# A convolution mixer's layer norm: four channel blocks added on VectorE before one product with ones, and one small load moved to ScalarE's queue

## The chip, the cores and the metric

The kernel runs on one core of one Trainium2 chip. The metric is the device time of one launch in microseconds (us). Names used below: TensorE (PE; its weight loads are PEld), VectorE (DVE), ScalarE (ACT), GpSimd (POOL) and SyncE (SP, which issues most DMAs). Every engine works through its own queue of instructions strictly in order and waits on semaphores for the others.

## The reference, cut to what matters

Two decoder layers over 256 tokens of width 1024. Each has four mixers on one projection of the normed input, then a feed-forward part (dense in layer 0, eight routed experts in layer 1). The change touches the fourth mixer, a gated depthwise convolution over 512 channels with a layer norm behind it:

```
def _conv_mixer(za, zg, w, bias, ln_g, ln_b):
    y = za * jax.nn.sigmoid(zg)
    y = lax.conv_general_dilated(y, w[:, None, :], window_strides=(1,), ...)   # 31 causal taps
    y = y + bias
    return jax.nn.silu(_layer_norm(y, ln_g, ln_b))

def _layer_norm(x, g, b):
    xc = x - jnp.mean(x, axis=-1, keepdims=True)
    y = xc * lax.rsqrt(jnp.mean(xc * xc, axis=-1, keepdims=True) + EPS)
    return y * g + b
```

The means run over the 512 channels of a token.

## The kernel before, in words

All large products are float32 by three passes: an operand is split into a rounded high part and a remainder, and `mm3` (lines 196 to 198) issues high by high, high by low and low by high. Weights come in pieces of 1 MB: SP issues the DMA into `raw` (line 163), ScalarE makes the high part `wh` (line 164), VectorE the low part `wl` (line 171), which is 128x2048 and waits for `wh`. There are three buffers each of `wh` and `wl`, so ScalarE starts a new `wh` only when TensorE has done with an older piece. `fill()` loads pieces until three are ahead of the products, and `get()` calls it.

Three engines, PE, ACT and DVE, run in the order in which the program issues their instructions. Beside the products of a layer's mixers run small generators ("threads"): `products()` gets its piece first, and so puts that piece's `wh` and `wl` on the queues of ScalarE and VectorE, and after every second `kk` it calls `tick()`, which lets each thread issue its next step and pops some convolution taps (line 503, VectorE, 128x256 each). `conv_norm` is such a thread. It waits until all taps are issued and then works on `cacc`, which holds the convolution as 128 channels by 4 blocks by 256 tokens:

1. the sum over all 512 channels as four products of `ones` with the four blocks, added up in the PSUM tile `cs` (line 757); ScalarE scales it to `cmean` (line 759); VectorE subtracts it (line 760); ScalarE squares into `c2` (line 762);
2. four ticks later the same four products on the squares (line 766), from which ScalarE makes `csd` (line 768);
3. two ticks later VectorE takes the reciprocal (line 770), scales (lines 771, 773), ScalarE takes a tanh (line 775), and after two more steps `oh` and `ol`, the split result, are made (lines 214, 215).

Around it run `merge(1, 1, gt)` (products on `oh`, `ol` of another mixer, then lines 697 and 698 on VectorE), `gates()` (products on the normed input `hh`, `hl`, then the tanh `gt` of line 685 on ScalarE) and `merge(0, ...)`. PSUM tiles of these products, `zps`, rotate over four buffers, so a later `gates()` starts when ScalarE has read an older tile into `gt`. In layer 1 the same code runs again some 536 us later.

At the start of the kernel SP loads the two halves of the first token tile `x_sb` (line 83), and GpSimd's queue loads `col`, the column vectors of both layers (gains, biases, taps; 128x320, line 89), then `pos_i` (line 91) and `inv` (line 93). TensorE transposes `x_sb` with `ident` (line 243), VectorE multiplies by the gain in `col` to give `xg` (line 261), and ScalarE and VectorE split that for the first products.

Of the kernel before, what the change touches and what calls it, by code (L numbers as in the profile page):

```python
# [11 lines left out]
F32 = mybir.dt.float32  # L12
# [4 lines left out]
OP = mybir.AluOpType  # L17
AX = mybir.AxisListType
# [3 lines left out]
P = 128  # L22
D = 1024
S = 256
# [40 lines left out]
def trunk(ctx: ExitStack, tc: tile.TileContext, x, pos, invf, rows, cols, wst, w_a, w_kvf, w_gate, w_br,  # L65
          w_out, f_g, f_u, f_d, router, e_g, e_u, e_d, gfin, out):
    nc = tc.nc
# [18 lines left out]
    ident = const.tile([P, P], F32, name="ident")  # L86
    make_identity(nc, ident)
    col = dconst.tile([P, L, NCOL], F32, name="col")
    nc.gpsimd.dma_start(col, cols)
    pos_i = const.tile([P, NT], I32, name="pos_i")  # L90
    nc.gpsimd.dma_start(pos_i, pos.rearrange("o (t p) -> p (o t)", p=P))
    inv = dconst.tile([P, HD // 2], F32, name="inv")
# [2 lines left out]
    ones = const.tile([P, P], F32, name="ones")  # L95
# [116 lines left out]
    def split(hi, lo, src, scale=None):  # L212
        if scale is None:
            nc.scalar.activation(hi, src, AF.Copy)  # L214
            nc.vector.tensor_sub(lo, src, hi.bitcast(F32))  # L215
        else:
            nc.scalar.activation(hi, src, AF.Copy, scale=scale)
            nc.vector.scalar_tensor_tensor(lo, src, scale, hi.bitcast(F32), op0=OP.mult, op1=OP.subtract)
# [126 lines left out]
    def mixers(l, mine, head, following):  # L345
        with ExitStack() as c2:
            mp = c2.enter_context(tc.tile_pool(name=f"mp{l}", bufs=1, reuse_waits="tile"))
            wk = c2.enter_context(tc.tile_pool(name=f"wk{l}", bufs=2, reuse_waits="tile"))
            bp = c2.enter_context(tc.tile_pool(name=f"bp{l}", bufs=8, reuse_waits="tile"))
            pmm = c2.enter_context(tc.tile_pool(name=f"pmm{l}", bufs=4, space=PSUM, reuse_waits="tile"))  # L350
            psm = c2.enter_context(tc.tile_pool(name=f"psm{l}", bufs=4, space=PSUM, reuse_waits="tile"))

            def big(name, shape=(P, NT, W), dtype=F32):

                n = int(np.prod(shape[1:]))
                tl = bp.tile([P, 1056], dtype, tag="big", name=name)[:shape[0], :n]
                if len(shape) == 3:
                    return tl.rearrange("p (a b) -> p a b", a=shape[1])
                if len(shape) == 4:
                    return tl.rearrange("p (a b c) -> p a b c", a=shape[1], b=shape[2])  # L360
                return tl
# [132 lines left out]
            cacc = mp.tile([P, 4, S], F32, name="cacc")  # L494
# [78 lines left out]
            def new_oT(n):  # L573
                hi = mp.tile([P, 4, S], F32R, name="oh", tag="oh", bufs=2)
                lo = mp.tile([P, 4, S], F32R, name="ol", tag="ol", bufs=2)
                oT[n] = (hi, lo)
                return hi, lo
# [171 lines left out]
                    yield 1  # L749


            def conv_norm():
                while taps:
                    yield 1
                ps = psm.tile([P, S], F32, tag="sm", name="cs")
                for b in range(4):
                    nc.tensor.matmul(ps, ones, cacc[:, b], start=b == 0, stop=b == 3)
                mean = wk.tile([P, S], F32, name="cmean", tag="o")
                nc.scalar.activation(mean, ps, AF.Copy, scale=1.0 / W)
                nc.vector.tensor_tensor(cacc, cacc, mean[:, None, :].to_broadcast([P, 4, S]), OP.subtract)  # L760
                c2_ = big("c2", (P, 4, S))
                nc.scalar.activation(c2_, cacc, AF.Square)
                yield 4
                ps = psm.tile([P, S], F32, tag="sm", name="cs")
                for b in range(4):
                    nc.tensor.matmul(ps, ones, c2_[:, b], start=b == 0, stop=b == 3)
                sd = wk.tile([P, S], F32, name="csd", tag="o")
                nc.scalar.activation(sd, ps, AF.Sqrt, bias=epsc, scale=1.0 / W)
                yield 2
                nc.vector.reciprocal(sd, sd)  # L770
                nc.vector.tensor_tensor(cacc, cacc, sd[:, None, :].to_broadcast([P, 4, S]), OP.mult)
                for b in range(4):
                    nc.vector.tensor_scalar(cacc[:, b], cacc[:, b], col[:, l, C_CG + b:C_CG + b + 1],
                                            col[:, l, C_CBB + b:C_CBB + b + 1], op0=OP.mult, op1=OP.add)
                nc.scalar.activation(c2_, cacc, AF.Tanh, scale=0.5)
                yield 2

                nc.vector.tensor_scalar(c2_, c2_, 1.0, 0.5, op0=OP.add, op1=OP.mult)
                nc.vector.tensor_mul(cacc, cacc, c2_)
                yield 1  # L780
                while 1 in oT:
                    yield 1
                oh, ol = new_oT(3)
                split(oh, ol, cacc)
# [74 lines left out]
            merge(1, 1, gt)  # L859
            del oT[1]  # L860
            start(conv_norm())
            for dc in range(2):
                gt = gates()
# [186 lines left out]
    def experts(l, mine):  # L1050
# [3 lines left out]
        with ExitStack() as c2:  # L1054
# [379 lines left out]
            with tc.If(nc.values_load(over_i[0:1, NE:NE + 1], min_val=0, max_val=1) > 0):  # L1434
# [8 lines left out]
    heads = [Normed(col[:, 0, C_MIX:C_MIX + KD]), Normed(col[:, 0, C_FFN:C_FFN + KD]),  # L1443
             Normed(col[:, 1, C_MIX:C_MIX + KD]), Routed(1)]
    mixers(0, heads[0], heads[1], [f_g[0, 0, h] for h in range(2)])
    dense_ffn(0, heads[1], heads[2], [w_a[1, CA, h] for h in range(2)])
    mixers(1, heads[2], heads[3], [e_g[0, 0, 0], e_g[0, 0, 1], e_u[0, 0, 0]])
    dense_ctx.close()
    experts(1, heads[3])
# [68 lines left out]
```

## Time and profile before

| what | value |
|---|---|
| three runs | 1726.6, 1728.15, 1728.6 us; median 1728.15 |
| the profiled execution | 1726.18 us, span 1724.4 us |
| PE busy | 1675.1 us, 97% of the span |
| PEld busy | 1215.4 us, 70% |
| DVE busy | 1054.3 us, 61% |
| ACT busy | 830.5 us, 48% |
| POOL busy | 12.1 us, 1% |
| bytes moved | 497.69 MB, mean 289 GB/s |
| granted TensorE clock, mean | 0.989 |

Times in the rows count from the start of the span; the profiled execution's own time has 1.8 us around the span. A duration is from an instruction's start to its end; neighbours on one engine overlap a little at their ends, so the step from one start to the next says what an instruction takes of the engine's time. A bracket at the end of a row holds the idle time of that engine before the instruction and what ended it.

### The profile page before, as it was taken

How to read it: one execution, taken by the hardware profiler on the slowest of the kernel's cores; microseconds unless marked ns; L12 is line 12 of the kernel's file. 1: busy time of each engine (PE TensorE's matmuls, PEld its weight loads, DVE VectorE, ACT ScalarE, POOL GpSimd, SP SyncE). 2: the span in 40 equal slices, each digit the busy share in tenths (PEclk: the TensorE clock that was granted, in tenths of full speed). 3: DMA queues.
4: the chain of work that ended last, by engine and by line, in shares of the span. 5: the costliest groups of instructions: out<-in, count | busy, mean ns of one | idle time of the engine just before them, and what ended most of it. 6: DMA issues, size and time to landing. Idle time of an engine off the chain costs nothing.

```text
span 1724.4 us, 20366 instructions
## 1 busy us (share of the span) xinstructions
PE 1675.1 (97%) x7800; PEld 1215.4 (70%) x7800; DVE 1054.3 (61%) x1282; ACT 830.5 (48%) x884; POOL 12.1 (1%) x28
## 2 busy tenths in 40 slices
PE   8999999999999999999999999999999999999996
PEld 6888888888887888888776565656656565655652
DVE  6779976555545678986675455536456544735534
ACT  6656454544434566445474444435444443534433
POOL 1000000000000000000000000000000000000000
PEclk9999999999999999999899999999999999999998
DMA  7444445555553643454668999999999999999996
GB/s 274 171 147 146 172 149 193 196 185 181 176 190 123 244 147 123 171 183 175 277 244 322 421 421 422 421 421 418 416 421 421 421 421 421 421 421 421 421 397 231
DMA packets 77818, 497.69 MB, mean 289 GB/s; under 512 B 8752, under 2 KB 8800, under 8 KB 20368
## 3 DMA queue, kind: packets, MB, share of 16 engines
q1 hardware_dynamic: 76752, 493.45, 72.8%
q0 software_dynamic: 960, 2.85, 0.6%
q8 instruction: 63, 1.03, 0.2%
q14 instruction: 43, 0.35, 0.1%
HBM read 495.22 MB, written 1.05 MB: 288 GB/s over the span
## 4 chain that ended last, share of the span: by engine, by line
PE 47%; DMA 9%; DVE 4%; ACT 3%; issue 1%; ACTq 0%; SPq 0%; DVEq 0%
DMA raw<-in_e_d 5%; PE yps L1302 4%; PE gps L1302 4%; PE ups L1302 3%; PE zps L196 3%; PE zps L198 3%; PE zps L197 3%; PE gps L196 3%; PE gps L197 3%; PE yps L197 3%; DVE wl L171 3%; PE gps L198 2%; PE yps L196 2%; PE yps L198 2%; ACT wh L164 2%; PE ups L196 2%
## 5 line engine op out<-in xcount | busy, mean ns | idle before, releaser
L171 DVE TENSOR_TENSOR wl<-raw,wh 128x2048 fp32r<-128x2048 f32 (+1 forms) x312 | 681.9, 2195 | 342.4 <-ACT wh L164 342.2
L164 ACT ACTIVATE wh<-raw 128x2048 fp32r<-128x2048 f32 (+1 forms) x312 | 571.1, 1838 | 406.1 <-PE zps L198 76.4
L196 PE MATMUL zps<-wh,hh 128*128 128x512 f32 (+1 forms) x544 | 215.7, 397 | 2.9 <-ACT wh L214 1.7
L197 PE MATMUL zps<-wl,hh 128*128 128x512 f32 (+1 forms) x544 | 209.5, 385 | 0.9 <-DVE wl L215 0.9
L198 PE MATMUL zps<-wh,hl 128*128 128x512 f32 (+1 forms) x544 | 209.6, 385 | 0.0
L215 DVE TENSOR_TENSOR al<-ps_t,ah 128x512 fp32r<-128x512 f32 x42 | 28.4, 688 | 181.0 <-ACT ah L214 180.8
L196 PEld LDWEIGHTS zps<-wh,hh 128*128 128x128 f32 x544 | 102.7, 189 | 23.7 <-ACT wh L214 2.1
L1372 ACT ACTIVATE act<-gps 128x512 f32<-128x512 f32 x42 | 25.1, 598 | 195.0 <-PE gps L1302 171.7
L197 PEld LDWEIGHTS zps<-wl,hh 128*128 128x128 f32 x544 | 102.7, 189 | 21.4 <-DVE wl L215 2.5
L198 PEld LDWEIGHTS zps<-wh,hl 128*128 128x128 f32 x544 | 102.5, 188 | 20.7
L1302 PE MATMUL ups<-rawn,xs 128*64 128x512 f32 x448 | 101.6, 597 | 1.6 <-DMA rawn<-in_e_u 1.6
L503 DVE SCALAR_TENSOR_TENSOR cacc<-ypad,col,cacc 128x256 f32<-128x256 f32 x240 | 101.4, 478 | 0.0
L1302 PE MATMUL yps<-rawn,aT 128*64 128x512 f32 x448 | 100.3, 596 | 0.0
L1302 PE MATMUL gps<-rawn,xs 128*64 128x512 f32 x448 | 100.3, 596 | 0.0
L197 PE MATMUL yps<-wl,ah 128*128 128x512 f32 x224 | 91.4, 408 | 6.7 <-DVE wl L171 6.5
L196 PE MATMUL yps<-wh,ah 128*128 128x512 f32 x224 | 92.0, 411 | 2.0 <-ACT wh L164 2.0
L196 PE MATMUL ups<-wh,xb 128*128 128x512 f32 x224 | 91.6, 409 | 0.0
L197 PE MATMUL gps<-wl,xb 128*128 128x512 f32 x224 | 88.8, 397 | 2.2 <-DVE wl L171 2.0
L198 PE MATMUL yps<-wh,al 128*128 128x512 f32 x224 | 90.4, 404 | 0.0
L196 PE MATMUL gps<-wh,xb 128*128 128x512 f32 x224 | 90.1, 402 | 0.0
L198 PE MATMUL ups<-wh,xb 128*128 128x512 f32 x224 | 88.6, 395 | 0.0
L198 PE MATMUL gps<-wh,xb 128*128 128x512 f32 x224 | 88.4, 394 | 0.0
(311 smaller groups left out, 2408.6 us busy)
## 6 DMA issues: line engine op xcount, KB each, us to landing
raw<-in_e_g SPq DMA_DIRECT2D x56, 1024.0 KB, 13.6
raw<-in_e_u SPq DMA_DIRECT2D x56, 1024.0 KB, 13.6
raw<-in_e_d SPq DMA_DIRECT2D x54, 1024.0 KB, 11.9
rawn<-in_e_g SPq DMA_DIRECT2D x52, 1024.0 KB, 12.7
rawn<-in_e_u SPq DMA_DIRECT2D x52, 1024.0 KB, 16.2
rawn<-in_e_d SPq DMA_DIRECT2D x52, 1024.0 KB, 14.1
raw<-in_w_gate SPq DMA_DIRECT2D x32, 1024.0 KB, 4.7
raw<-in_w_a SPq DMA_DIRECT2D x28, 1024.0 KB, 4.8
```

The source lines that it names most:

```text
L164: nc.scalar.activation(hi[:, sl], raw[:, sl], AF.Copy)
L171: nc.vector.tensor_sub(lo[:, sl], raw[:, sl], hi[:, sl].bitcast(F32))
L196: nc.tensor.matmul(ps, xh, wh, start=first, stop=False)
L197: nc.tensor.matmul(ps, xh, wl, start=False, stop=False)
L198: nc.tensor.matmul(ps, xl, wh, start=False, stop=last)
L215: nc.vector.tensor_sub(lo, src, hi.bitcast(F32))
L503: nc.vector.scalar_tensor_tensor(cacc[:, b], src, wcol, cacc[:, b], op0=OP.mult, op1=OP.add)
L1302: nc.tensor.matmul(ps[js], lhs(k)[:, js], w[:, kk], start=k == 0, stop=k == ktot - 1)
L1372: nc.scalar.activation(a, gps, AF.Silu)
```

## The change

A helper adds the four blocks on VectorE (one reduce over the block axis, from 128x256x4 to 128x256 into `cb`) and multiplies the result once by `ones`. Both sums of the norm use it. `cb` takes its buffer from the pair that `cmean` and `csd` use. The load of `col` is issued by ScalarE's queue in place of GpSimd's.

```diff
@@ -86,7 +86,7 @@
     col = dconst.tile([P, L, NCOL], F32, name="col")
-    nc.gpsimd.dma_start(col, cols)
+    nc.scalar.dma_start(col, cols)
@@ -749,21 +749,25 @@
+            def over_channels(a):
+
+                cb = wk.tile([P, S], F32, name="cb", tag="o")
+                nc.vector.tensor_reduce(cb, a.rearrange("p b s -> p s b"), axis=AX.X, op=OP.add)
+                ps = psm.tile([P, S], F32, tag="sm", name="cs")
+                nc.tensor.matmul(ps, ones, cb, start=True, stop=True)
+                return ps
+
             def conv_norm():
                 while taps:
                     yield 1
-                ps = psm.tile([P, S], F32, tag="sm", name="cs")
-                for b in range(4):
-                    nc.tensor.matmul(ps, ones, cacc[:, b], start=b == 0, stop=b == 3)
+                ps = over_channels(cacc)
                 mean = wk.tile([P, S], F32, name="cmean", tag="o")
...
                 yield 4
-                ps = psm.tile([P, S], F32, tag="sm", name="cs")
-                for b in range(4):
-                    nc.tensor.matmul(ps, ones, c2_[:, b], start=b == 0, stop=b == 3)
+                ps = over_channels(c2_)
                 sd = wk.tile([P, S], F32, name="csd", tag="o")
```

On TensorE the products with ones keep their places between the same two `zps` products: four instructions on `cacc` or `c2` become one on `cb`, and each of the two now waits for VectorE. What stands on VectorE there, in layer 0, before (`wl` is a piece's low part; `c_2022` is `c2`):

```order
L503 SCALAR_TENSOR_TENSOR cacc<-ypad,col,cacc 128x256 [waits DVE_49] x5
L171 TENSOR_TENSOR wl<-raw,wh 128x2048 [waits DMAHW2_49,PE_49,Activation_49]
L760 TENSOR_TENSOR cacc<-cacc,cmean 128x1024 [waits Activation_49]
L697 SCALAR_TENSOR_TENSOR gt<-gt,zps 128x512 [waits PE_49]
L698 TENSOR_TENSOR merged<-merged,gt 128x512 [waits DVE_49]
L697 SCALAR_TENSOR_TENSOR gt<-gt,zps 128x512 [waits PE_49]
L698 TENSOR_TENSOR merged<-merged,gt 128x512 [waits DVE_49]
L171 TENSOR_TENSOR wl<-raw,wh 128x2048 [waits DMAHW3_49,Activation_49]
L770 RECIPROCAL csd<-csd 128x256 [waits Activation_49]
```

The same stretch of VectorE's queue after the change (line numbers are now the changed file's: 755 is the reduce, 766 the subtraction that was 760, 774 the reciprocal that was 770):

```order
L503 SCALAR_TENSOR_TENSOR cacc<-ypad,col,cacc 128x256 [waits DVE_49] x5
L171 TENSOR_TENSOR wl<-raw,wh 128x2048 [waits DMAHW3_49,PE_49,Activation_49]
L755 TENSOR_REDUCE cb<-cacc 128x256 [waits DVE_49]
L766 TENSOR_TENSOR cacc<-cacc,cmean 128x1024 [waits DVE_49,Activation_49]
L697 SCALAR_TENSOR_TENSOR gt<-gt,zps 128x512 [waits PE_49]
L698 TENSOR_TENSOR merged<-merged,gt 128x512 [waits DVE_49]
L697 SCALAR_TENSOR_TENSOR gt<-gt,zps 128x512 [waits PE_49]
L698 TENSOR_TENSOR merged<-merged,gt 128x512 [waits DVE_49]
L171 TENSOR_TENSOR wl<-raw,wh 128x2048 [waits DMAHW4_49,Activation_49]
L755 TENSOR_REDUCE cb<-c_2021 128x256
L774 RECIPROCAL csd<-csd 128x256 [waits Activation_49]
```

Both reduces stand behind a `wl` that itself waits for ScalarE's `wh`. Layer 1 has the same rows. On ScalarE the instructions between the two sums and the `csd` keep their order; before, they were:

```order
L759 ACTIVATE cmean<-cs 128x256 [waits PE_49]
L762 ACTIVATE c_2022<-cacc 128x1024 [waits DVE_49]
L164 ACTIVATE wh<-raw 128x2048 [waits DMAHW3_49,PE_49,Activation_49]
L768 ACT_TABLE_LOAD
L768 ACTIVATE csd<-cs,epsc 128x256 [waits PE_49]
```

And on ScalarE after the change:

```order
L765 ACTIVATE cmean<-cs 128x256 [waits PE_49]
L768 ACTIVATE c_2021<-cacc 128x1024 [waits DVE_49]
L164 ACTIVATE wh<-raw 128x2048 [waits DMAHW4_49,PE_49,Activation_49]
L772 ACT_TABLE_LOAD [waits PE_49]
L772 ACTIVATE csd<-cs,epsc 128x256 [waits Activation_49]
```

The wait for TensorE's second sum has moved from the `csd` instruction to the load of its function table ahead of it. At the start of the kernel ScalarE's queue issues the load of `col` ahead of its first table load, and GpSimd's queue has one DMA less ahead of `pos_i`.

## Rows read from the trace of the kernel before

**Rows 1.** The page: busy tenths of the DMA engines in 40 slices of 43.1 us.
```profile
DMA  7444445555553643454668999999999999999996
```
**Rows 2.** Chain of waits, 750 to 790 us: start, us, engine and tile (layer 1).
```profile
759.17 1.73 PE cs L757 x8
```
**Rows 3.** Timeline 212 to 252 us, first sum: start, us, engine, line, operation.
```profile
220.49 2.06 DVE L503 SCALAR_TENSOR_TENSOR cacc<-ypad,col,cacc 128x256 f32<-128x256 f32 x5
...
222.58 0.40 PE L198 MATMUL zps<-wh,ol 128*128 128x512 f32 x1
...
222.82 1.89 PE L757 MATMUL cs<-cacc,ones 128*128 128x256 f32 x8
224.14 2.29 DVE L171 TENSOR_TENSOR wl<-raw,wh 128x2048 fp32r<-128x2048 f32 x1 [1.59 <-ACT wh L164]
...
224.35 0.58 PE L196 MATMUL zps<-wh,oh 128*128 128x512 f32 x1
...
224.74 0.38 ACT L759 ACTIVATE cmean<-cs 128x256 f32<-128x256 f32 x1 [0.64 <-PE cs L757]
...
226.35 1.22 DVE L760 TENSOR_TENSOR cacc<-cacc,cmean 128x1024 f32<-128x1024 f32 x1
```
**Rows 4.** Timeline 212 to 252 us, second sum.
```profile
228.98 1.92 ACT L164 ACTIVATE wh<-raw 128x2048 fp32r<-128x2048 f32 x1 [0.32 <-PE zps L198]
...
230.10 1.89 PE L766 MATMUL cs<-c,ones 128*128 128x256 f32 x8
230.91 1.28 ACT L768 ACT_TABLE_LOAD   x1
230.92 2.29 DVE L171 TENSOR_TENSOR wl<-raw,wh 128x2048 fp32r<-128x2048 f32 x1 [0.58 <-ACT wh L164]
...
232.21 0.48 ACT L768 ACTIVATE csd<-cs,epsc 128x256 f32<-128x256 f32 x1
...
233.13 1.75 DVE L770 RECIPROCAL csd<-csd 128x256 f32<-128x256 f32 x1
```
**Rows 5.** Timeline 228 to 262 us: where the norm's chain meets TensorE again.
```profile
246.98 1.25 ACT L685 ACTIVATE gt<-zps,rs 128x512 f32<-128x512 f32 x2
247.70 0.50 PE L196 MATMUL zps<-wh,hh 128*128 128x512 f32 x1 [0.58 <-ACT gt L685]
```
**Rows 6.** VectorE's groups: line, operation, count, busy us, mean ns, idle before.
```profile
L1026 DVE TENSOR_REDUCE rank<-cmp 128x8 f32<-128x128 f32 x3 | 0.9, 286 | 0.1
L1132 DVE TENSOR_REDUCE over<-tmp 128x8 f32<-128x64 f32 x1 | 0.2, 220 | 0.0
L760 DVE TENSOR_TENSOR cacc<-cacc,cmean 128x1024 f32<-128x1024 f32 x2 | 2.4, 1218 | 0.0
L778 DVE TENSOR_SCALAR c<-c 128x1024 f32<-128x1024 f32 x2 | 1.4, 686 | 0.0
```
**Rows 7.** TensorE's timeline: its two longest waits after the start, and products behind the first.
```profile
872.01 0.53 PE L1253 MATMUL gsps<-gts,dm 128*128 128x2 f32 x2 [3.78 <-DVE gts L1149]
872.41 0.77 PE L196 MATMUL ups<-wh,xb 128*128 128x512 f32 x1
...
875.11 0.58 PE L196 MATMUL ups<-wh,xb 128*128 128x512 f32 x1
...
1145.09 1.13 PE L1222 MATMUL gaps<-dm,hh 128*128 128x256 f32 x4 [2.93 <-DVE dm L1207]
```
**Rows 8.** Stretches: busy us of each engine, then PEclk, DMA share, GB/s.
```profile
872.00:874.00 2.00, 1.99 (x6) 1.70 (x7) 1.86 (x8) 1.93 (x2) 0.00 (x0) 0.52 0.00 0
...
1144.00:1148.00 4.00, 2.91 (x9) 2.55 (x10) 3.14 (x5) 0.76 (x3) 0.00 (x0) 0.64 1.02 424
```
**Rows 9.** Timeline 0 to 30 us: the load of col and who waits for it.
```profile
5.46 1.11 PE L243 MATMUL ps_t<-ident,x_sb 128*128 128x128 f32 x4 [0.72 <-DMA x_sb<-in_x]
...
6.37 1.29 DVE L261 TENSOR_TENSOR xg<-ps_t,col 128x512 f32<-128x512 f32 x2 [5.14 <-DMA col<-in_cols]
...
11.72 1.31 ACT L214 ACTIVATE wh<-raw 128x512 fp32r<-128x512 f32 x2 [1.40 <-DMA raw<-in_w_a]
```

## The prediction

> **What bounds the kernel now.** I read the page first. The table above has TensorE busy for 97% of the span, while the transfers fill the DMA engines only from about slice 22 of 40 on (the row of tenths reaches 9 there) [rows 1]. In the mixers, where the norm stands, the transfers run at about half, so TensorE's own order of work sets the pace: the chain of waits runs through its products there, the four products with ones of the norm's sum among them, at 1.73 us [rows 2]. What leaves TensorE's queue there is a gain, and what it has to wait for there is a loss. The timeline of the two sums in layer 0 is what decides. In the first, VectorE ends its last taps at 220.49 + 2.06 = 222.55, TensorE starts the sum at 222.82 without any wait (the row has no bracket), and VectorE then sits idle for 1.59 us because the next piece's low part has to wait for ScalarE [rows 3]. The second has the same picture at 230.10 [rows 4]. Layer 1 repeats both some 536.2 us later (its sum is the one in the chain), so every amount below counts twice.
>
> **What is removed.** Four float32 products with ones take 222.82 to 224.35 = 1.53 us of TensorE, 0.38 us each [rows 3]. Three of four go: 1.15 us per sum, 4.6 us over four sums. That is all that the change can save in the norm.
>
> **What the reduce costs VectorE.** No row reduces 1024 elements per partition. Two reduces are on record, 220 ns over 64 elements and 286 ns over 128, a slope of 1.03 ns for each further element: 286 + 896 x 1.03 = 1.21 us. The subtraction, 1024 elements from two operands, takes 1.218 us [rows 6]. I take 1.21 us, which both are nearest to. Below, a 1024-element operation with one operand took 0.69 us. Above, I allow twice the subtraction, 2.4 us, because the reduce steps 1 KB from one element to the next and no row shows that [rows 6].
>
> **Where it stands matters more than its price.** Both reduces are queued behind a `wl`, and TensorE, whose order is fixed, now waits for them.
>
> First sum: that `wl` cannot start before ScalarE's `wh`, and the next VectorE instruction starts at 226.35 [rows 3]. So the reduce runs 226.35 to 227.56, and TensorE, ready at 222.82, starts at 227.6. It waits 4.8 us, saves 1.15: later by 3.65 us. It can do nothing else meanwhile, as all following products are behind the sum in its queue.
>
> Second sum: ScalarE's `wh` at 228.98 was released by TensorE (the bracket), so it, and the `wl` behind it, move with TensorE: 3.65 us later. VectorE was through with that `wl` at 233.13, when the reciprocal starts [rows 4]; now at 236.8, and the reduce ends at 238.0. TensorE arrives at 230.10 + 3.65 = 233.75, waits 4.3, saves 1.15: another 3.15 us. The squares are ready long before, as the subtraction is done by about 230.0 and the square behind it by 231.1. TensorE is now 6.8 us late.
>
> **The norm's own chain.** The first sum's result reached ScalarE 0.58 us after its last product's start (224.74, against 222.82 + 7 x 0.19) [rows 3]. The second sum, now one product in two records, starts at 238.05, so the result is there at 238.8. Before, the table load of 1.28 us ran beside TensorE's sum; in the new order it carries the wait, so it runs 238.8 to 240.1, `csd` takes 0.48, and the reciprocal starts at 240.65 in place of 233.13 [rows 4]: 7.5 us later. Everything behind it, to `oh` and `gt`, keeps its durations. TensorE meets that chain at 247.70, where it had waited 0.58 us for `gt` [rows 5]. It would now come at 247.12 + 6.8 = 253.9 and find the first `gt`, which had been ready 0.05 ahead of 247.70, at 247.65 + 7.5 = 255.15. So at an unchanged clock a layer costs 7.5 us.
>
> **The clock.** Two long TensorE waits in the trace were 3.78 us (until 872.01) and 2.93 us (until 1145.09) [rows 7]. After the first, the granted clock is 0.52 over 872 to 874, that is, mostly the lower level, 1.2 GHz; 1144 to 1148 shows 0.64 [rows 8]. Seven products of 128x512 start from 872.41 to 875.11 [rows 7], six steps of 0.45 us, where at 2.4 GHz a step was 0.24 (222.58 to 222.82) [rows 3]: a loss of 7 x 0.2 = 1.4 us. The new waits, 4.8 and 4.3 us, are longer than either, so I count a fall behind each. The first fall delays TensorE and, through the release of `wh`, all of the second sum: the chain then gives `gt` at 255.15 + 1.4 = 256.55. The second delays TensorE alone: 253.9 + 2.8 = 256.7. TensorE is now just the later one, so its old wait of 0.58 us is gone, and a layer costs 256.7 - 247.70 = 9.0 us. Two layers: 18.0 us. Since either path alone gives nearly that, a second fall of half the size changes little.
>
> **The load of col.** VectorE's first `xg` waits 5.14 us for it, until 6.37 [rows 9]. If it lands early, the first `xg` may run at once, but the second still needs TensorE's transposes, which end at 5.46 + 1.11 = 6.57, where it had started about 0.65 after 6.37, at 7.0. The gain is at most 0.45 us. ScalarE's wait for `raw` at 11.72 is set by a transfer [rows 9] and may swallow it: 0. Against it, 160 KB now share the first microseconds with `x_sb`: at the mean of 289 GB/s in the table, about 0.6 us at worst. I take -0.3, nearest the upper limit of the gain since 5.14 us is so plainly the load's. The issue on ScalarE and its table load behind it are covered by that engine's idle start, and GpSimd's remaining loads come earlier, which nothing waits for.
>
> The Trainium skill, "DMA: Bandwidth & Descriptors", section "Issuing engines are not separate DMA queues", says that transfers share the same 16 DMA engines whichever engine issues them, and that another issuer saves only issue time; by that rule this term would be about 0 and the sum 18.0. No run here has tried it yet.
>
> **The sum.** 18.0 - 0.3 = 17.7 us on the profiled execution's 1726.18 = 1743.9. That execution is 1.97 us under the median of the runs, so against the median it is 1745.9. Nothing later gives it back: the dense part is bound by TensorE, and the experts' transfers, though full later, start as the end of the mixers releases their buffers.
>
> **The rivals.**
>
> *The clock holds* (waits on VectorE are as computed, but TensorE stays at 2.4 GHz behind them). For: the sums' products are only part of the work. Against: both rows of waits above. 2 x 7.5 - 0.3 = 14.7, so 1742.9. Chance 0.15.
>
> *The reduce is slow over its long step.* At 2.4 us each of the four reduces adds 1.2 us to both paths: 4.8 more, 22.5 in all, 1750.7. For: no row has such a step; against: none shows such a loss. Chance 0.13. The Trainium skill, "SBUF — State Buffer", section "Door 1: The DMA port swizzle", notes that SBUF is read in lines of 16 bytes and that accesses which each go to a new line pay a penalty; it gives no size for it, and every element here is on a new line, so by that rule this rival would be the outcome.
>
> *Half is absorbed.* If the experts' full DMA engines [rows 1], not the end of layer 1's mixers, set the end, layer 1's 9.0 us vanish: about +8.7, 1736.9. Against: the engines are at 4 to 6 tenths while layer 1's mixers end. Chance 0.07.
>
> *Faster: VectorE is never late.* If VectorE ran far enough ahead to end the reduce before 222.82 + 1.15 = 223.97, the removed products decide: 4 x 1.15 + 0.3 = 4.9 less, 1723.2. It has 1.59 us of idle time there [rows 3], enough for the reduce, but the `wl` stands in front. Chance 0.03. That the cost and the saving cancel (within 0.2%) gets 0.02.
>
> **How the numbers follow.** The forecast has 0.60, at 1745.9. About 0.2%, 3.5 us, is what a measurement of this kernel can tell from no change. Faster than that 0.03, within it 0.03, slower 0.94. The range goes from 1738, below the clock rival with a reduce at its lower end (a chain shorter by 2 x 2 x 0.52 = 2.1, so 1740.8) and short of the absorbed case, up to 1753, past the slow reduce with one more fall that lasts twice as long (1.4).
>
> **What would show it.** A reduce of about 1.2 us on VectorE directly behind a `wl`, four times; TensorE's products on `cb` with waits of about 4.8 and 4.3 us for VectorE in each layer; a granted clock near 0.5 for some 3 us behind them; the table load directly behind the second sum; no wait for `gt` at the end of the chain. It is wrong if those products start without waiting, if the reduce takes over 2 us, if the clock stays at 1.0, or if the experts start 18 us later and yet end at the old time. For the load: the first `xg` starts near 4.9 and the first `zps` product before 8.3.

## The result and the profile after

The changed kernel takes 1750.74 us (median of 4 runs, 1749.75 to 1751.17) against 1728.08 us for the kernel before: a ratio of 1.0134, 95% interval 1.0122 to 1.0147, so 22.7 us slower. The forecast was 1745.9 us, in a range of 1738 to 1753: right in its sign and in its path, 4.8 us short in size. The changed kernel's profiled execution took 1749.75 us with a span of 1748.1; the mean granted clock fell from 0.989 to 0.982.

The page's row of busy time hides the loss: TensorE is busy 4.8 us longer than before, though twelve products with `ones` have gone, and its share of the span falls only to 96%.

```profile
PE 1679.9 (96%) x7776; PEld 1217.0 (70%) x7776; DVE 1062.3 (61%) x1286; ACT 830.9 (48%) x884; POOL 12.4 (1%) x27
```

TensorE's list of waits shows it at once. The first row is new, and the wait for `gt` of [rows 5] is no longer in the list (columns: engine, tile and line that waited, what it waited for, us in all, times, longest):

```profile
PE cs L757 <- DVE cb L755: 20.6, 4, 5.4
PE yps L197 <- DVE wl L171: 6.9, 6, 1.8
```

The timeline of the first sum in layer 0 (start, us, engine, line, operation; the bracket is the idle time before) answers to [rows 3]:

```profile
223.77 2.29 DVE L171 TENSOR_TENSOR wl<-raw,wh 128x2048 fp32r<-128x2048 f32 x1 [1.59 <-ACT wh L164]
...
225.98 1.88 DVE L755 TENSOR_REDUCE cb<-cacc 128x256 f32<-128x1024 f32 x1
...
228.00 1.19 PE L757 MATMUL cs<-cb,ones 128*128 128x256 f32 x2 [5.39 <-DVE cb L755]
...
228.63 0.99 PE L196 MATMUL zps<-wh,oh 128*128 128x512 f32 x1
...
229.42 0.63 PE L197 MATMUL zps<-wl,oh 128*128 128x512 f32 x1
...
233.69 0.46 PE L198 MATMUL zps<-wh,ol 128*128 128x512 f32 x1
...
233.99 0.39 PE L196 MATMUL zps<-wh,oh 128*128 128x512 f32 x1
```

VectorE is idle for 1.59 us, exactly as before the change, because the `wl` in front waits for `wh`. Only then does it run the `wl`, and only then the reduce, which takes 1.88 us. TensorE stands for 5.39 us. Behind the wait its products take 0.63 us instead of 0.39, until 233.7.

The second sum repeats it (answers to [rows 4]):

```profile
235.62 1.92 ACT L164 ACTIVATE wh<-raw 128x2048 fp32r<-128x2048 f32 x1 [3.66 <-PE zps L198]
...
237.56 2.29 DVE L171 TENSOR_TENSOR wl<-raw,wh 128x2048 fp32r<-128x2048 f32 x1 [0.58 <-ACT wh L164]
...
239.77 1.88 DVE L755 TENSOR_REDUCE cb<-c 128x256 f32<-128x1024 f32 x1
...
241.80 1.19 PE L757 MATMUL cs<-cb,ones 128*128 128x256 f32 x2 [4.91 <-DVE cb L755]
...
243.07 1.28 ACT L772 ACT_TABLE_LOAD   x1 [5.54 <-PE cs L757]
...
244.87 1.75 DVE L774 RECIPROCAL csd<-csd 128x256 f32<-128x256 f32 x1 [3.22 <-ACT csd L772]
```

The windows of 4 us show the clock (busy us of PE, PEld, DVE, ACT, POOL; then granted clock, DMA share, GB/s):

```profile
224.00:228.00 4.00, 0.00 (x0) 0.03 (x1) 3.85 (x2) 0.00 (x0) 0.00 (x0) 0.87 0.32 76
228.00:232.00 4.00, 4.00 (x10) 3.14 (x11) 1.43 (x2) 1.44 (x2) 0.00 (x0) 0.50 0.55 225
232.00:236.00 4.00, 4.00 (x15) 3.23 (x14) 1.60 (x3) 0.38 (x1) 0.00 (x0) 0.77 0.00 0
```

In 228 to 232 the clock is 0.50, the lower level of 1.2 GHz: the product on `cb` (two records) and eight others start in those 4 us, and 13 start in the next 4, at 0.77 (the view counts 15, with two that were still running). TensorE had stood for 5.39 us before. In layer 1 the waits are 5.40 and 4.89 us, with 0.57 over 776 to 780 and 0.50 over 788 to 792. The slow stretch behind a wait of the same length is shorter there:

```profile
776.93 1.19 PE L757 MATMUL cs<-cb,ones 128*128 128x256 f32 x2 [5.40 <-DVE cb L755]
...
780.02 0.40 PE L198 MATMUL zps<-wh,ol 128*128 128x512 f32 x1
```

From the sum's start to the first product at full speed it takes 3.1 us in layer 1 (776.93 to 780.02) and 6.0 in layer 0 (228.00 to 233.99).

The product that waited for `gt` at 247.70 [rows 5] now starts, without a wait, 12.47 us later; in layer 1 its twin is 23.23 us late (the first row is from the kernel before, the other two from the changed one):

```profile
783.90 0.50 PE L196 MATMUL zps<-wh,hh 128*128 128x512 f32 x1 [0.59 <-ACT gt L685]
...
260.17 0.39 PE L196 MATMUL zps<-wh,hh 128*128 128x512 f32 x1
...
807.13 0.50 PE L196 MATMUL zps<-wh,hh 128*128 128x512 f32 x1
```

So the two layers' mixers hold 23.2 of the 23.7 us by which the span grew; nothing later gives it back.

### The profile page after: what moved, and what is told of

Read it like the earlier page. It is cut to its first block, busy times and chain, and to the rows that moved or that the text cites. A ratio compares the mean times of both kernels' runs of the same rounds, so it can differ in the third digit from the quotient of the medians.

```text
span 1748.1 us, 20324 instructions
## 1 busy us (share of the span) xinstructions
PE 1679.9 (96%) x7776; PEld 1217.0 (70%) x7776; DVE 1062.3 (61%) x1286; ACT 830.9 (48%) x884; POOL 12.4 (1%) x27
## 4 chain that ended last, share of the span: by engine, by line
PE 40%; DMA 12%; DVE 6%; ACT 4%; issue 1%; ACTq 0%; SPq 0%; DVEq 0%
DMA raw<-in_e_d 6%; DMA raw<-in_e_g 4%; DVE wl L171 4%; PE yps L1306 4%; PE gps L1306 3%; ACT wh L164 3%; PE gps L197 2%; PE gps L196 2%; PE yps L197 2%; PE gps L198 2%; PE zps L196 2%; PE yps L198 2%; PE yps L196 2%; PE zps L197 2%; PE zps L198 2%; PE ups L196 2%
```

## The experiments

Nine kernels ran. Each diff is against the changed kernel unless it says otherwise.

**The load alone** (e1_col_only): the kernel before, with only this line changed.

```diff
-    nc.gpsimd.dma_start(col, cols)
+    nc.scalar.dma_start(col, cols)
```

> Only the load of col is moved to ScalarE's queue; both sums of the norm stay four products. If the load's part is what the changed kernel's timeline suggests (its first taps ran 0.37 us earlier than before), the time is the kernel before's less about 0.4 us, some 1727.7 us, and the first xg on VectorE starts near 5.6 instead of 6.4. If the load is hidden anyway, the time is the kernel before's within 0.1 us. If the new queue costs something elsewhere (a part of the 22.7 us), the time is above the kernel before's.

Measured: 1726.66 us (11 runs), ratio 0.9991, interval 0.9981 to 1.0. That is 1.2 us less than the 1727.82 of its comparison, but the interval reaches up to no change. Its trace has TensorE at the first sum 0.6 us earlier than in [rows 3] (222.20 against 222.82), and the first `xg` starts at 5.58 as expected. The load costs nothing, so the norm is the whole loss.

**The step of the reduce** (e2_groups_of_neighbours): the reduce adds four neighbours instead of four elements 1 KB apart.

```diff
-                nc.vector.tensor_reduce(cb, a.rearrange("p b s -> p s b"), axis=AX.X, op=OP.add)
+                nc.vector.tensor_reduce(cb, a.rearrange("p b s -> p (b s)").rearrange("p (s b) -> p s b", b=4),
+                                        axis=AX.X, op=OP.add)
```

> The changed kernel with the reduce reading four neighbouring elements for each sum instead of four that lie 1 KB apart; the sums are of other elements than the norm's, the size of the operation is the same. If the step of 1 KB is what makes the reduce 1.88 us long, it falls to about 1.2 us and four waits get 0.67 us shorter: about 1748.0 us. If the operation costs that with groups of four whatever the step, the reduce stays at 1.88 us and the time at 1750.7 us.

Measured: the reduce takes 1.21 us (ns as min, median, max; first and last start), and TensorE's four waits sum to 17.9 us.

```profile
L755 DVE TENSOR_REDUCE cb<-cacc x2: 1211/1212/1214, 226.3 to 772.4; 128x256 f32<-128x1024 f32 x2
```

In the changed kernel the same view says

```profile
L755 DVE TENSOR_REDUCE cb<-cacc x2: 1877/1878/1880, 226.0 to 774.9; 128x256 f32<-128x1024 f32 x2
```

so the long step costs 0.67 us per reduce. Its time, 1913.03 us, says nothing of the change: the sums are of other elements, so the experts get other inputs, and more pieces of weights are worked through (354 low parts in place of 312). Ahead of the experts both kernels do the same work, and there e2 is ahead: the `cmp` that ranks layer 1's experts first starts at 862.4 us against 865.8, 3.4 us earlier, where four times 0.67, or 2.7, had been expected.

**Two additions instead of the reduce** (e3_two_adds).

```diff
-                nc.vector.tensor_reduce(cb, a.rearrange("p b s -> p s b"), axis=AX.X, op=OP.add)
+                two = wk.tile([P, W], F32, name="two", tag="half", bufs=3).rearrange("p (b s) -> p b s", b=2)
+                nc.vector.tensor_add(two, a[:, 0:2], a[:, 2:4])
+                nc.vector.tensor_add(cb, two[:, 0], two[:, 1])
```

> The changed kernel with the reduce replaced by two adds on VectorE at the same place (512, then 256 elements per partition, 0.69 + 0.42 us by the kernel before's rows). If TensorE's four waits end with VectorE's work behind the split of the piece, each is 0.75 us shorter: 3.0 us in all, about 1747.7 us, still some 20 us over the kernel before because the place in the queue is the same. If the choice of operation were the whole cost, the time would fall to near the kernel before's 1728 us.

Measured: 1746.82 us, ratio 1.0108 (1.0093 to 1.0124). The additions take 0.69 and 0.42 us, and the waits shrink by about the difference, 0.7 us each; four of them remain:

```profile
PE cs L759 <- DVE cb L757: 17.7, 4, 4.7
```

A cheaper sum in the same place mends little: 3.9 of the 22.7 us by the medians.

**Products on nothing during the wait** (e4_products_while_waiting): ahead of each product on `cb`, twelve products into the same PSUM tile that it overwrites. They keep TensorE busy while it would stand.

```diff
+                for _ in range(12):
+                    nc.tensor.matmul(ps, ones, fmask.rearrange("p a k -> p (a k)"), start=True, stop=True)
                 nc.tensor.matmul(ps, ones, cb, start=True, stop=True)
```

> The changed kernel with 12 more products of ones with a constant tile (128x256 float32, about 0.38 us each at the full clock, 4.6 us) ahead of each of the four sums, so that TensorE works through most of its waits of 5.4 and 4.9 us; their results are overwritten. If the granted clock falls because TensorE idles there, it now stays at 1.0, the products behind the sums run 0.23 us apart at once, and what is left is the wait and the norm's own chain: about 7.5 + 1.3 = 8.8 us per layer, 17.3 us over the kernel before in all, about 1745.4 us. If the clock has no part in it, the time stays at 1750.7 us; if the added products themselves delay the sums, it rises above.

Measured: 1744.46 us, ratio 1.0094 (1.0079 to 1.011). The wait is filled by products that nobody uses, the granted clock is 1.00 through every window from 222 to 250, and the wait for `gt` is back, longer than in [rows 5]:

```profile
222.11 5.34 PE L758 MATMUL cs<-fmask,ones 128*128 128x256 f32 x24
...
225.64 1.92 DVE L755 TENSOR_REDUCE cb<-cacc 128x256 f32<-128x1024 f32 x1
...
227.61 0.70 PE L759 MATMUL cs<-cb,ones 128*128 128x256 f32 x2 [0.16 <-DVE cb L755]
...
255.93 0.50 PE L196 MATMUL zps<-wh,hh 128*128 128x512 f32 x1 [1.33 <-ACT gt L685]
```

The first sum is made about as late as in the changed kernel (227.61 against 228.00), and still the time is 6.3 us lower (6.0 with each kernel set against its own comparison). That is what the slow stretches behind the four waits cost in the end.

**The reduce ahead of the low part** (e5_ahead_of_the_split): price and operation unchanged; the first reduce is issued with the last tap, the second one tick ahead of its product.

```diff
+                def last_tap():
+                    tap(3, TAPS - 1)
+                    add_blocks(cacc)
...
+                taps[-1] = last_tap
...
-                ps = over_channels(cacc)
+                ps = over_channels()
...
-                yield 4
-                ps = over_channels(c2_)
+                yield 3
+                add_blocks(c2_)
+                yield 1
+                ps = over_channels()
```

> Both reduces are kept, but the first is issued right behind the last taps, ahead of the low part wl that stood in front of it, and the second one tick earlier, ahead of the second wl. Theory (the wait comes from the reduce's place in VectorE's queue, not from its price): the first reduce runs about 222.6 to 224.5, so TensorE waits about 1.6 us for it and saves 1.15 us of products; the second is ready before TensorE comes. The granted clock stays near 1.0. The low parts and the reciprocal are pushed back by up to 1.9 us, so the wait for gt grows to about 2 to 3 us in each layer: in all 1730 to 1734 us. Rival (the price of the reduce or the single product as such is what costs, wherever it stands): still near 1750 us.

Measured: 1735.67 us, ratio 1.0041 (1.0026 to 1.0057), 1.7 us above the range expected. It is 8.4 us over its comparison (1727.29), where the changed kernel was 22.7 over: some 14 us are gone by moving an instruction that costs the same.

```profile
222.26 1.93 DVE L762 TENSOR_REDUCE cb<-cacc 128x256 f32<-128x1024 f32 x1
...
224.12 2.28 DVE L171 TENSOR_TENSOR wl<-raw,wh 128x2048 fp32r<-128x2048 f32 x1
...
224.34 0.67 PE L768 MATMUL cs<-cb,ones 128*128 128x256 f32 x2 [1.68 <-DVE cb L762]
...
230.73 0.70 PE L768 MATMUL cs<-cb,ones 128*128 128x256 f32 x2 [0.17 <-DVE cb L762]
...
233.24 2.29 DVE L171 TENSOR_TENSOR wl<-raw,wh 128x2048 fp32r<-128x2048 f32 x1
...
250.00 0.50 PE L196 MATMUL zps<-wh,hh 128*128 128x512 f32 x1 [3.45 <-ACT gt L690]
```

The waits for the sums are 1.68 and 0.17 us, nearly as expected. What was put too low is the push behind them: the second reduce moves the `wl` to 233.24, and the reciprocal behind it to 235.44, 2.3 us later than in [rows 4]. So `gt` is late, TensorE stands 3.45 us for it where 2 to 3 had been expected, and the clock, which was to stay near 1.0, falls there (0.50 over 252 to 254). Of the 20.6 us of waits at the four sums 3.7 are left, and 6.9 us of new waits for `gt` have come in.

**Splitting the norm's result later** (e6_split_later): against the kernel before, with the load on ScalarE's queue.

```diff
                 nc.vector.tensor_mul(cacc, cacc, c2_)
-                yield 1
+                yield 4
                 while 1 in oT:
```

> The load of col on ScalarE's queue and the old sums of four products; the high and low part of the norm's result are made three ticks later, behind the gt that TensorE waits for. Theory (the wait of 0.58 us for gt comes from oh standing ahead of it on ScalarE): that wait is gone in both layers, about 1.2 us less than with the load alone (1726.7), 1725.4 us. Rival (that wait is set elsewhere, or TensorE then waits for oh): no change against the load alone.

Measured: 1725.58 us (11 runs), ratio 0.9987 (0.9978 to 0.9996). Against its own comparison (1727.29) that is 1.7 us less, where the load alone gave 1.2: the times do not tell the two apart. The trace does show that the wait for `gt` is out of TensorE's list in both layers, and that `gt` now runs ahead of `oh`, at 242.23 instead of 246.98.

**Both sums early, products later** (e7_sums_without_waits): two additions as in e3, the first pair with the last tap, the products one and two ticks later.

```diff
+                yield 1
+                ps = over_channels()
...
-                yield 4
-                ps = over_channels(c2_)
+                yield 3
+                add_blocks(c2_)
+                yield 2
+                ps = over_channels()
...
                 nc.scalar.activation(c2_, cacc, AF.Tanh, scale=0.5)
-                yield 2
+                yield 4
```

> The sums on VectorE are issued early enough that TensorE need not wait: two additions (128x512, then 128x256) in place of the reduce, for the first sum with the last taps, and the product with ones a tick later; for the second one tick ahead of the product and that a tick later too; the split of the norm's result three ticks later. Theory (the idea of the change is sound, its place in the queues is not): no wait of TensorE for VectorE at the sums, the clock stays near 1.0, and the three products saved per sum show: 4 x 1.15 us plus the 2 x 0.58 us of the gt wait plus 0.4 us of the load, so 1721 to 1723 us, faster than before. Rival (the additions only push the low parts and the gt behind them back): TensorE waits for gt or wl, 1727 us or more.

Measured: 1735.23 us, ratio 1.0048 (1.0034 to 1.0062): slower than before, a miss. The later split was put at the tanh in this kernel, by two ticks and not three, so the scaling behind the tanh is later too. The first sum does what was expected, without a wait at 223.95. The second does not:

```profile
230.24 2.29 DVE L171 TENSOR_TENSOR wl<-raw,wh 128x2048 fp32r<-128x2048 f32 x1 [0.28 <-ACT wh L164]
...
232.45 0.68 DVE L763 TENSOR_TENSOR two<-c 128x512 f32<-128x512 f32 x1
...
233.17 0.42 DVE L764 TENSOR_TENSOR cb<-two 128x256 f32<-128x256 f32 x1
...
233.74 0.88 PE L770 MATMUL cs<-cb,ones 128*128 128x256 f32 x2 [2.34 <-DVE cb L764]
...
239.16 2.29 DVE L171 TENSOR_TENSOR wl<-raw,wh 128x2048 fp32r<-128x2048 f32 x1 [5.57 <-ACT wh L164]
...
241.37 1.75 DVE L790 RECIPROCAL csd<-csd 128x256 f32<-128x256 f32 x1
```

By its tick the second pair is behind a `wl` again, and the reciprocal, two ticks later than before, has slipped behind the next `wl`: VectorE stood idle for 5.57 us until 239.16, although the reciprocal's input was ready at 236.47 (`csd` runs from 236.00 for 0.47 us). What stands behind that is late as well, and TensorE waits for a `wl` once more in each layer:

```profile
PE zps L197 <- DVE wl L171: 4.7, 2, 2.4
```

With 4.7 us at the second sums and 1.4 for `gt`, the new waits come to 10.8 us, against 4.6 us of products saved, and the clock falls behind one of them. That is most of the 9.7 us by which e7 is slower than e6.

**Only the first sum** (e8_first_sum_only): e6 with the first pair of additions and its product as in e7; the second sum keeps its four products and its tick. The diff is against the kernel before and leaves out what it shares with e6 and e7.

```diff
-                ps = psm.tile([P, S], F32, tag="sm", name="cs")
-                for b in range(4):
-                    nc.tensor.matmul(ps, ones, cacc[:, b], start=b == 0, stop=b == 3)
+                yield 1
+                ps = over_channels()
...
-                yield 4
+                yield 3
                 ps = psm.tile([P, S], F32, tag="sm", name="cs")
```

> The kernel with the later split (1725.6 us), and of the two sums only the first is made on VectorE: two additions behind the last taps, in the 1.6 us in which VectorE stands idle there, and the product with ones a tick later; the second sum keeps its four products, at the same tick as before. Theory (a sum on VectorE pays where VectorE has a gap ahead of TensorE's arrival): TensorE does not wait for it and saves 1.15 us in each layer, so 1723.3 us; the clock stays near 1.0. Rival (what TensorE saves is taken back by a wait behind it, as the additions delay the low part by 0.4 us): no change, 1725.6 us.

Measured: 1722.57 us (9 runs), ratio 0.9971 (0.9961 to 0.9981); 0.7 us under what was expected.

```profile
222.30 0.69 DVE L763 TENSOR_TENSOR two<-cacc 128x512 f32<-128x512 f32 x1
...
223.03 0.43 DVE L764 TENSOR_TENSOR cb<-two 128x256 f32<-128x256 f32 x1
...
223.87 2.29 DVE L171 TENSOR_TENSOR wl<-raw,wh 128x2048 fp32r<-128x2048 f32 x1 [0.41 <-ACT wh L164]
...
223.94 0.59 PE L770 MATMUL cs<-cb,ones 128*128 128x256 f32 x2
```

The additions fill 1.2 of the 1.59 us in which VectorE had stood idle; 0.41 are left, so the `wl` is not later for them.

**Both sums in gaps** (e9_both_sums_in_gaps): e8, and the second pair is issued by a hook in front of the next piece, not at a tick; product two ticks later than the four were, reciprocal one tick behind it, and the scaling behind the tanh back at its old tick.

```diff
+            ahead = []
...
                 got = []
+                while ahead:
+                    ahead.pop(0)()
...
+                ahead.append(lambda: add_blocks(c2_))
+                yield 5
+                ps = over_channels()
...
-                yield 2
+                yield 1
                 nc.vector.reciprocal(sd, sd)
...
                 nc.scalar.activation(c2_, cacc, AF.Tanh, scale=0.5)
-                yield 2
+                yield 1
```

> As the run with the first sum alone, and the second sum too on VectorE: its two additions are issued ahead of the low part of the piece that follows (by a hook at the start of the products, not at a tick), its product with ones two ticks later than the four products were, the reciprocal at the next tick, still ahead of the low part behind it. Theory: additions until about 231.1, TensorE arrives at about 231.4 and does not wait; the reciprocal starts near 233.8, where it stood before; another 1.15 us in each layer, so 1721.0 us. Rival (the second place has no room: the low part, pushed back by 0.8 us, or the table load that waits for the later sum in front of wh makes TensorE wait): 1723 us or more, with TensorE's waits for wl, wh or gt grown.

Measured: 1720.41 us (5 runs), ratio 0.996 (0.9946 to 0.9974), 7.1 us faster than the kernel before and 30 us faster than the changed one.

```profile
229.42 0.69 DVE L767 TENSOR_TENSOR two<-c 128x512 f32<-128x512 f32 x1
...
230.14 0.42 DVE L768 TENSOR_TENSOR cb<-two 128x256 f32<-128x256 f32 x1
...
230.49 2.29 DVE L171 TENSOR_TENSOR wl<-raw,wh 128x2048 fp32r<-128x2048 f32 x1
...
230.79 0.60 PE L774 MATMUL cs<-cb,ones 128*128 128x256 f32 x2
...
233.27 1.75 DVE L793 RECIPROCAL csd<-csd 128x256 f32<-128x256 f32 x1 [0.50 <-ACT csd L791]
```

TensorE waits for neither sum, and the reciprocal starts at 233.27, where it stood before the change (233.13). The second sum's own share, 2.2 us against e8, is about the 2.3 expected, though the two intervals overlap. A new wait of 0.28 us for `wl` in each layer takes some of it.

## Why the prediction was right in kind and short in size

- **Removed: 1.15 us per sum.** Right. It could not show in the changed kernel; in e8 and e9, where little takes it back, each sum brings, by the medians, 1.1 to 1.5 us per layer.
- **The reduce, 1.21 us.** This term failed. It took 1.88 us, between the value taken and the upper bound of 2.4. The 1.21 us are what the same reduce takes over neighbours (e2); the long step adds 0.67 us, or 2.7 us over four. The rule that had been weighed against it, the Trainium skill, "SBUF — State Buffer", section "Door 1: The DMA port swizzle", has accesses to new lines of SBUF pay a penalty: the traces agree, with 0.67 us over 1024 elements. Only these two steps were tried, so what else could make a long step slow stays open. That rival's time, 1750.7, equals the result only by chance: it had the reduce at 2.4 us and the clock too cheap.
- **The place in the queue.** Right: both reduces behind a `wl`, and waits of 5.39 and 4.91 us where 4.8 and 4.3 had been worked out; the 0.6 us more in each are nearly the 0.67 us of the reduce. e5 shows that the place counts for more than the price: the same reduce elsewhere costs some 14 us less, even with a new wait.
- **The norm's chain.** Right. With the clock held up, e4 has TensorE waiting 1.33 us for `gt`; the prediction's terms for that case gave 255.15 less 253.9, or 1.25. The table load of 1.28 us is directly behind the second sum, and the old wait for `gt` is gone in the changed kernel.
- **The clock.** The mechanism was right, the size not: 3.0 us in the sum (18.0 less 2 x 7.5), 6.3 us by e4. The step that failed is "a loss of 7 x 0.2 = 1.4 us" for each fall, taken from one fall behind a wait of 3.78 us. Behind the four waits, in order of time, ten, ten, three and six steps from product to product are 0.43 us instead of 0.23. The sum's own product is slow as well: from its start to the second product behind it takes 1.42 us, in e8 0.66. That is 29 x 0.2 + 4 x 0.76 = 8.8 us of TensorE's time, 2.2 for each fall. Without the falls TensorE would have stood 1.33 us per layer for `gt`, as in e4; less that, 6.1 us are left, close to e4's 6.3. As TensorE was the later of the two paths already, all that the falls are longer shows in the time. Why equal waits had unequal falls stays open.
- **The load of col.** -0.3 forecast, -1.2 measured by e1's medians (interval from -3.3 to 0); the traces have TensorE at the first sum 0.4 us earlier in the changed kernel and 0.6 in e1. The load lands 3.7 us after its issue from ScalarE's queue, where from GpSimd's the same view has 4.9, and is issued 0.56 us earlier (0.82 against 1.38). The first `xg`, at 5.58, no longer waits for it but for TensorE, and the first `zps` product starts at 7.51. It had been said that the first `xg` starts near 4.9, but the first half of `x_sb` now lands later, so that the transposes start at 4.46 instead of 3.66.

The terms close: 17.7 + 2.7 (reduce) + 3.3 (clock) - 0.9 (load) = 22.8, against 22.7 measured. So close a fit is partly luck, as the load's part is known no better than to a microsecond or two.

The words ahead of the forecast have the first sum beside `merge(1, 1)`; its products belong to `merge(0, 0)`, and the second sum to the `gates()` behind it. No term rests on that.

## What to carry to other kernels

Moving work from the engine that bounds to an idler one paid here only where the work was issued in a gap of that engine, before the bound engine arrives: a busy share of 61% says nothing about what stands in front of the instruction. Look for the gap in the timeline, count what is queued ahead, and follow what the new instruction pushes back (the low part and the reciprocal in e5 and e7) to the next place where the bound engine meets that chain. And a wait costs more than its length where the clock falls behind it.

## What was not expected of the hardware

- A wait on TensorE of 2.34 us was followed by a fall of the clock in one place and by none in another. In e7 the second sum waits 2.34 us in both layers; behind it the granted clock is 0.52 over 234 to 236 in layer 0, and stays at 1.00 in layer 1. The 1.68 us of e5 brought no fall. Nor was there a fall behind the waits of 2.38 and 2.36 us for `wl` in e7 (1.00 over 262 to 268 and 802 to 808). What decides it was not tried.
- The same load of 160 KB takes 1.2 us less from issue to landing on ScalarE's queue than on GpSimd's (3.7 against 4.9 us). The Trainium skill, "DMA: Bandwidth & Descriptors", section "Issuing engines are not separate DMA queues", says that starting DMAs on several engines at once saves only the sequencer's time for starting them. The rows show more: of the 1.2 us the issuing instruction is shorter by 0.26 (0.40 against 0.66 us), and the start 0.56 us earlier comes on top. Where the rest comes from was not tried.
